# Modulation pieces, attention's small steps and buffer slots re-placed in a one-core hybrid block

## The chip, the cores and the metric

The kernel runs on one core of a Trainium2 chip. A core has a matrix engine (TensorE: PE for its matmuls, PEld for its weight loads), a vector engine (DVE), a scalar engine (ACT), GpSimd (POOL), and SyncE (SP), whose queue issues nearly all DMAs here. The metric is the device time of one execution, in microseconds (us); less is better.

## What is computed

One block of a hybrid model on 256 tokens of width 2048, in float32:

```python
mod = silu(c) @ ada_w + ada_b            # 6 x 2048: sh1, sc1, g1, sh2, sc2, g2
h = rmsnorm(x, norm1_g) * (1 + sc1) + sh1
z = h @ w_in                             # q, six k/v parts, gates, lx, ly, ga, gb
o_a = nsa_attention(q, ...)              # 16 heads, 4 kv groups, q * HEAD_DIM ** -0.5
o_b = gelu(ly) * rg_lru(causal_dwconv(lx), ...)
merged = sigmoid(ga) * (o_a @ proj_a) + sigmoid(gb) * (o_b @ proj_b)
x = x + g1 * (merged @ w_out)
h = rmsnorm(x, norm2_g) * (1 + sc2) + sh2
x = x + g2 * conv_glu_ffn(h, ffn_up, ..., ffn_down)
return rmsnorm(x, final_g)
```

Attention has three parts, weighted by sigmoid gates: over 15 compressed blocks, over selected blocks, and over a window. With 256 tokens the selection takes in all blocks and the window all tokens, so both are causal softmax attention with keys of their own.

## The kernel before, in words

**Dense products.** Every weight matrix comes in pieces of 128 x 2048 float32 (1 MB) into one of four `raw` buffers (`stage`, L97). `split` (L102) makes two halves of it, each as a rounded high part (ACT, L107) and the rest as a low part (DVE, L108), into `hi` and `lo` buffers of which there are three each. PE multiplies high by high, high by low and low by high. `dense_pair` (L114, matmuls L130), `dense_shift` (L135), `dense_pair1` (L172, matmuls L185, L187, L188) and `dense_tok` (L192, matmuls L203 to L205) are four forms of it. All loads go through `load` (L52) in program order on SP's queue, and a `raw` buffer is loaded again when DVE has read it.

**Modulation.** A column of `mod` for 128 outputs is the product of a 1 MB piece of the transposed `ada_w` with the row `crow`, summed over the row: one DVE instruction over 2048 elements. The first 32 pieces (sh1, sc1) are made at the start by `ada1_next` (L306, L323); the very first (`ada0`) is 32 small matmuls instead (L318). The other 64 stand in the list `fill` (L513: g1, then sc2, sh2, g2) and are taken off it by `filler` (L515), which runs `ada_piece` (L232: one load through a `raw` buffer, one product on DVE in L234, one addition in L235). Where the calls of `filler` stand in the program decides when that work comes.

```python
720  # lx loop, 8 passes:          filler(2)
773  # recurrence's gate, 8:       filler(2 if pr % 4 == 0 else 0)
797  # merge, n = 0..3, two sides: filler(2 if n == 0 else 4)
810  # behind merge:               filler(max(0, len(fill) - 16))
902  # feed-forward, first half:   filler(2 if gr > 5 else 1 if gr > 1 else 0)
```

**Stages, by time in the profile.** Norm and first columns (0 to 20 us); the projections for keys, values, queries and two gate blocks (L527 to L569, to about 240 us), whose outputs are collected in four spans of the contraction: the first span is copied out by ACT (L478), the others are added by DVE (L480); compression of keys and values (`gather`, `compress`); attention (L632), eight units of one group and one half of the tokens, between the last query projections and the lx loop (285 to 475 us); the recurrence with its gate (L725 to L773, to about 590 us); merge (L781 to L809): gates and two projections, four column tiles each; the output projection (L839 to L855, about 895 to 985 us), four tiles, each with its rows of x, a transposition and the scaled copies for the second norm; the feed-forward part.

**A unit of attention.** For the compressed part: scores, softmax in small DVE steps, transposition to `pcT` (L661). Then four heads, each: scores for both key sets in one PSUM tile `s` (two buffers, L667), the causal mask added by a matmul (L670), row maxima (DVE, L676), times -SCALE (L677), two exponentials on ACT with their sums (L679), the sums clamped (L681), inverted (L682) and times the gate (L683), the probabilities scaled (L686), turned by PE (L689) through one PSUM tile `tp` (tag "t", one buffer) and copied out by ACT (L691). At the end the products with the values (L693, L697) and the copy to `oA`.

**What orders the work.** The program is written stage by stage, but the order of the instructions on each engine is laid by a planner that simulates the program; `split` and `reduce` have raised priority. Tiles with the same tag share a slot, and a new tile waits for the last reader of the old one. `big` has slots B0, B1, C0 to C7, D0 to D5, M0 and M1; `tmp` has small ones (`xp`, `r`, `iu`, `u`, `tt`, `pv1`, `sm`).

Of the kernel before, what the change touches and what calls it, by code (L numbers as in the profile page):

```python
# [5 lines left out]
F32 = mybir.dt.float32  # L6
# [8 lines left out]
D = 2048  # L15
# [23 lines left out]
def block_kernel(tc, x_t, x_n, gf_row, cols_d, consts_d, ada_w, w_kv0, w_kv, w_v, w_gate, w_q, cmp_w, cmp_w2,  # L39
# [16 lines left out]
    with ExitStack() as es:  # L56
# [191 lines left out]
        ada0 = stage(ada_w[1, 0])  # L248
        ada1_raw = stage(ada_w[0, 0])
# [56 lines left out]
        def ada1_next():  # L306
            if not ada1:
                return
            with ExitStack() as behind:
# [4 lines left out]
                if kt == 0 and m == 1:  # L314

                    pa = psx.tile([128, 512], F32, tag="t", bufs=1, name="pa")
                    for j in range(KT):
                        PE.matmul(pa[:, 0:1], ada0[:, j * 128:j * 128 + 128], csil[:, j:j + 1], start=(j == 0),  # L318
                                  stop=(j == KT - 1))
# [38 lines left out]
        w2t = tmp.tile([128, 2, 128], F32, tag="xp", bufs=2, name="w2t")  # L358
# [22 lines left out]
        def gather(j, pos):  # L381

            parts = []
            for a in range(2):
                g = big.tile([128, 16, 4, NCMP], F32, tag="C6", name="gat")
# [3 lines left out]
                for n in range(2):  # L389
                    q = big.tile([128, 8, 2, 60], F32R, tag="C%d" % (2 + 2 * a + n), name="gath")  # L390
                    v = g[:, 8 * n:8 * n + 8].rearrange("p b g n -> p b (g n)")
                    A.activation(q[:, :, 0], v, AF.Copy)
                    V.tensor_tensor(q[:, :, 1], v, q[:, :, 0].bitcast(F32), op=ALU.subtract)
                    parts.append(q)
            return psx.tile([128, 512], F32, tag="s", bufs=2, name="cp"), parts

        def compress(j, cp, half):
# [16 lines left out]
            hs = tmp.tile([128, 4, 64], F32, tag="xp", bufs=2, name="hs")  # L414
# [21 lines left out]
        KV, TOK = range(4), range(8, 12)  # L436
# [31 lines left out]
        def out_of(i, ps, q):  # L468
            if i < 2 and q < 3:
                return  # L470
            for j in range(2):
# [5 lines left out]
                if q == 0 or i < 2:  # L477
                    A.activation(d, v, AF.Copy)  # L478
# [153 lines left out]
        def attention(g, t):  # L632
# [14 lines left out]
            A.activation(pc, pc, AF.Exp, scale=SCALE)  # L647
# [16 lines left out]
            nj = 2 * (t + 1)  # L664
            for hh in range(4):
# [5 lines left out]
                if hh == 0:  # L671
                    p = big.tile([128, 512], F32, tag="C3", name="p")
                else:
                    p = tmp.tile([128, 512], F32, tag=("r", "iu", "tt")[hh - 1], bufs=1, name="p")
                sm = tmp.tile([128, 6], F32, tag="sm", bufs=2, name="sm")
                V.tensor_reduce(sm[:, 0:2], s[:, 0:2 * nk].rearrange("p (b n) -> p b n", b=2), axis=AX, op=ALU.max)  # L676
                V.tensor_scalar(sm[:, 0:2], sm[:, 0:2], -SCALE, None, op0=ALU.mult)  # L677
                for b in range(2):
                    A.activation(p[:, b * nk:b * nk + nk], s[:, b * nk:b * nk + nk], AF.Exp, bias=sm[:, b:b + 1],  # L679
                                 scale=SCALE, accum_out=sm[:, 2 + b:3 + b])  # L680
                V.tensor_scalar(sm[:, 2:4], sm[:, 2:4], 1e-30, None, op0=ALU.max)  # L681
                V.reciprocal(sm[:, 2:4], sm[:, 2:4])  # L682
                V.tensor_tensor(sm[:, 4:6], sm[:, 2:4], gates[:, hh, 1:3], op=ALU.mult)  # L683
                for b in range(2):
                    pb = p[:, b * nk:b * nk + nk]
                    V.tensor_scalar(pb, pb, sm[:, 4 + b:5 + b], None, op0=ALU.mult)  # L686
                tp = psx.tile([128, 512], F32, tag="t", bufs=1, name="tp")
                for j in range(nj):
                    PE.transpose(tp[:, j * 128:j * 128 + 128], p[:, j * 128:j * 128 + 128], ident)  # L689
                for n in range(t + 1):  # L690
                    A.activation(pT[n][:, :, hh, :], tp[:, n * 256:n * 256 + 256].rearrange("p (j q) -> p j q", q=128),  # L691
                                 AF.Copy)
# [21 lines left out]
        for pr in range(8):  # L714
# [5 lines left out]
            filler(2)  # L720
# [4 lines left out]
        for bt in range(4):  # L725
# [37 lines left out]
            for h in range(2):  # L763
# [9 lines left out]
                filler(2 if pr % 4 == 0 else 0)  # L773
# [7 lines left out]
        for n in range(4):  # L781
            m = []
            for s, rhs in ((0, lambda kt: oA[:, kt]), (1, lambda kt: oB[kt // 2][:, kt % 2])):
# [3 lines left out]
                else:  # L787
                    ps = dense_tok([w_gates[n - 1, s, k] for k in range(4)], h1r)
# [4 lines left out]
                ps = dense_tok([w_proj[n, s, k] for k in range(4)], rhs)  # L793
# [3 lines left out]
                filler(2 if n == 0 else 4)  # L797
# [12 lines left out]
        filler(max(0, len(fill) - 16))  # L810
# [12 lines left out]
        for n in range(8):  # L823
            sh = modc[:, 48 + 2 * n:50 + 2 * n].unsqueeze(2).to_broadcast([128, 2, 2])
            A.activation(hp[n][:, :, 0, 256:258], sh, AF.Copy)
            V.tensor_tensor(hp[n][:, :, 1, 256:258], sh, hp[n][:, :, 0, 256:258].bitcast(F32), op=ALU.subtract)

# [11 lines left out]
        for n in range(4):  # L839
            ps = dense_tok([w_out[n, k] for k in range(4)], lambda kt: mg[kt // 2][:, kt % 2])  # L840
# [13 lines left out]
            if n == 1:  # L854
                tc.keep_in_program_order(A.activation(warm, col("eps"), AF.Sqrt))  # L855
        rstd(sdev, sums)
        dr = tmp.tile([128, 2, 128], F32, tag="xp", bufs=2, name="dr")
# [16 lines left out]
        for half in range(2):  # L874
# [3 lines left out]
            for gr in range(12):  # L878
                take = up(gr, 0, half)
                for f in range(2):  # L880
                    b = half * 24 + gr * 2 + f
                    gp = tmp.tile([128, 256], F32, tag="xp", bufs=2, name="gp")
# [137 lines left out]
```

## Time and profile before

| | us |
|---|---|
| median of 3 runs | 1792.68 |
| lowest, highest | 1792.08, 1794.26 |
| the profiled execution | 1793.77 |
| its span in the profile, first to last instruction | 1792.0 |
| PE busy | 1771.6 (99%) |
| PEld, DVE, ACT busy | 1545.9 (86%), 1350.5 (75%), 881.9 (49%) |
| read from HBM | 425.72 MB, 239 GB/s over the span |

Busy time is the time in which at least one instruction of an engine runs. Matmuls are pipelined: a row's duration is longer than the distance to the next start, and it is that distance (the pitch) that tells how fast PE goes. A wait is put down to the instruction that came last.

### The profile page before, as it was taken

What the parts mean: (1) busy time and instruction counts of PE and PEld (TensorE: products, weight loads), DVE (VectorE), ACT (ScalarE), POOL (GpSimd) and SP (SyncE); (2) the same over time, 40 slices, a digit from 0 to 9 for tenths busy, and PEclk for the clock granted to TensorE, in tenths of its full rate; (3) what the DMA queues carried; (4) which work ended last, traced back from release to release, by engine and by line L of the source; (5) the groups of instructions that cost most, each with busy time, mean ns of one, the idle gap of its engine ahead of it and who ended that gap; (6) DMA issues with size and microseconds to landing.
All of it is one profiled execution on the core that took longest, in us unless ns stands there. A gap on an engine that the chain in (4) does not pass through costs nothing.

```text
span 1792.0 us, 25746 instructions
## 1 busy us (share of the span) xinstructions
PE 1771.6 (99%) x10262; PEld 1545.9 (86%) x10262; DVE 1350.5 (75%) x1976; ACT 881.9 (49%) x1202; POOL 0.2 (0%) x4
## 2 busy tenths in 40 slices
PE   8999999999999999999999999999999999999997
PEld 7999898888999888888888998888888888888886
DVE  7998897998698766767765997888555677766555
ACT  5644464655578444444445644444433444444443
POOL 0000000000000000000000000000000000000000
PEclk9999999999999999999999999999999999999999
DMA  9999864665646867777775566777655555555552
GB/s 350 379 335 355 288 245 161 235 212 203 221 173 227 303 237 290 286 292 281 294 266 195 186 235 235 282 282 282 239 193 200 191 188 188 188 188 188 190 198 106
DMA packets 64200, 429.50 MB, mean 240 GB/s; under 512 B 7088, under 2 KB 7376, under 8 KB 15568
## 3 DMA queue, kind: packets, MB, share of 16 engines
q1 hardware_dynamic: 63792, 427.08, 66.2%
q8 instruction: 80, 1.31, 0.3%
q10 hardware_dynamic: 288, 0.79, 0.1%
q14 instruction: 40, 0.33, 0.1%
HBM read 425.72 MB, written 2.11 MB: 239 GB/s over the span
## 4 chain that ended last, share of the span: by engine, by line
PE 86%; DVE 6%; DMA 4%; issue 2%; ACT 2%; SPq 0%; DVEq 0%; ACTq 0%
PE P L130 26%; PE P L204 12%; PE P L205 12%; PE P L203 12%; PE P L187 3%; PE P L188 3%; PE P L185 3%; DMA raw<-ada_w 2%; DVE lo L108 2%; PE P L464 2%; PE P L466 2%; PE P L465 2%; PE P L149 1%; PE P L148 1%; PE P L150 1%
## 5 line engine op out<-in xcount | busy, mean ns | idle before, releaser
L107 ACT ACTIVATE hi<-raw 128x1024 fp32r<-128x1024 f32 x588 | 622.0, 1060 | 764.5 <-PE P L205 325.5
L108 DVE TENSOR_TENSOR lo<-raw,hi 128x1024 fp32r<-128x1024 f32 x588 | 717.1, 1222 | 370.5 <-ACT hi L107 369.7
L130 PE MATMUL P<-h,hi 128*128 128x512 f32 x1344 | 463.9, 394 | 0.0
L130 PE MATMUL P<-h,lo 128*128 128x256 f32 x1344 | 366.4, 278 | 0.0
L130 PEld LDWEIGHTS P<-h,hi 128*128 128x128 f32 x1344 | 249.1, 188 | 54.9
L130 PEld LDWEIGHTS P<-h,lo 128*128 128x128 f32 x1344 | 252.4, 188 | 4.2
L234 DVE SCALAR_TENSOR_TENSOR raw<-raw,crow 128x2048 f32<-128x2048 f32 x64 | 146.2, 2285 | 3.6 <-DMA raw<-ada_w 3.2
L188 PE MATMUL P<-h,lo 128*128 128x256 f32 x512 | 147.6, 289 | 0.8 <-DVE lo L108 0.8
L187 PE MATMUL P<-h,hi 128*128 128x256 f32 x512 | 146.7, 287 | 0.0
L185 PE MATMUL P<-h,hi 128*128 128x256 f32 x512 | 146.7, 287 | 0.0
L464 PE MATMUL P<-h,hi 128*128 128x256 f32 x384 | 107.9, 285 | 0.3 <-ACT hi L107 0.3
L465 PE MATMUL P<-h,hi 128*128 128x256 f32 x384 | 107.6, 284 | 0.0
L466 PE MATMUL P<-h,lo 128*128 128x256 f32 x384 | 102.2, 284 | 0.0
L188 PEld LDWEIGHTS P<-h,lo 128*128 128x128 f32 x512 | 97.8, 191 | 1.8 <-DVE lo L108 1.4
L187 PEld LDWEIGHTS P<-h,hi 128*128 128x128 f32 x512 | 97.9, 191 | 1.4 <-issue 1.2
L185 PEld LDWEIGHTS P<-h,hi 128*128 128x128 f32 x512 | 97.9, 191 | 1.0 <-issue 0.7
L204 PE MATMUL P<-lo,ua 128*128 128x512 f32 x240 | 93.5, 390 | 0.3 <-DVE lo L108 0.3
L205 PE MATMUL P<-hi,ua 128*128 128x512 f32 x240 | 93.4, 389 | 0.0
L203 PE MATMUL P<-hi,ua 128*128 128x512 f32 x240 | 83.6, 389 | 0.0
L204 PE MATMUL P<-lo,h 128*128 128x512 f32 x192 | 75.5, 393 | 0.0
L464 PEld LDWEIGHTS P<-h,hi 128*128 128x128 f32 x384 | 74.0, 193 | 1.1 <-ACT hi L107 0.5
L205 PE MATMUL P<-hi,h 128*128 128x512 f32 x192 | 74.9, 390 | 0.0
(281 smaller groups left out, 3131.6 us busy)
## 6 DMA issues: line engine op xcount, KB each, us to landing
raw<-ada_w SPq DMA_DIRECT2D x96, 1024.0 KB, 5.0
raw<-w_up SPq DMA_DIRECT2D x96, 1024.0 KB, 4.8
raw<-w_down SPq DMA_DIRECT2D x48, 1024.0 KB, 4.9
raw<-w_lru SPq DMA_DIRECT2D x32, 1024.0 KB, 4.9
raw<-w_proj SPq DMA_DIRECT2D x32, 1024.0 KB, 5.1
raw<-w_gates SPq DMA_DIRECT2D x24, 1024.0 KB, 6.5
raw<-w_out SPq DMA_DIRECT2D x16, 1024.0 KB, 4.9
raw<-w_kv SPq DMA_DIRECT2D x24, 512.0 KB, 6.7
```

Of the source, the lines that this page charges most:

```text
L107: A.activation(hi[:, :n], raw[:, lo_col:lo_col + n], AF.Copy)
L108: V.tensor_tensor(lo[:, :n], raw[:, lo_col:lo_col + n], hi[:, :n].bitcast(F32), op=ALU.subtract)
L130: PE.matmul(ps[f][:, 0:256] if w else ps[f], hl[w][:, k * 256 + f * 128:k * 256 + f * 128 + 128], r[:, 0:256] if w else r, start=(kt == 0 ...
L185: PE.matmul(o, hi[:, sl], r[:, 0:256], start=(kt == 0 and f == 0), stop=False, skip_group_check=True)
L187: PE.matmul(o, hi[:, sl], r[:, 256:512], start=False, stop=False, skip_group_check=True)
L188: PE.matmul(o, lo[:, sl], r[:, 0:256], start=False, stop=(kt == n - 1), skip_group_check=True)
L203: PE.matmul(ps[j], xh, hi[:, w], start=(kt == 0), stop=False, skip_group_check=True)
L204: PE.matmul(ps[j], xh, lo[:, w], start=False, stop=False, skip_group_check=True)
L205: PE.matmul(ps[j], xl, hi[:, w], start=False, stop=(kt == n - 1), skip_group_check=True)
L234: V.scalar_tensor_tensor(raw, raw, 1.0, row, op0=ALU.mult, op1=ALU.mult, accum_out=modc[:, c:c + 1])
L464: PE.matmul(o, hi[:, sl], h1[:, kt, 0:256], start=first and f % 2 == 0, stop=False, skip_group_check=True)
L465: PE.matmul(o, hi[:, sl], h1[:, kt, 256:512], start=False, stop=False, skip_group_check=True)
```

## The change

- `ada0` and `ada1_raw` no longer use `raw` buffers: they get D0, D1 and D5 (the slots of the first queries and of the values), and `ada0` is loaded in two halves.
- `cmpb`, `gat` and `gath` change slots; `w2t` and `hs` become the two halves of one tile, as do the two `gp` of the feed-forward part (tag "xp", now one buffer of the same total size).
- Queries are multiplied by SCALE as they are copied out; the factor leaves the three exponentials and the maxima, whose sign comes from the reduction.
- In attention the clamp, the inversion and the gate are done for two heads at a time, and the scaling, turning and copying of both heads follows.
- `filler` is called elsewhere: `dense_tok` takes a list `fills` of piece numbers behind which one piece is made. The 64 pieces lie so, before and after: lx loop 16 and 4, recurrence's gate 4 and 0, merge 28 and 36, output projection 0 and 8, feed-forward part 16 and 16.
- The shift copies (L823 to L826) move behind the output projection's loop.

```diff
-        def dense_tok(pieces, lhs, late=None):
+        def dense_tok(pieces, lhs, late=None, fills=()):
...
                     for j in range(2):
                         products(j, k0, *hl)
+                if ip in fills:
+                    filler()
...
-        ada0 = stage(ada_w[1, 0])
-        ada1_raw = stage(ada_w[0, 0])
+        ada0 = [big.tile([128, 1024], F32, tag="D%d" % n, name="ada0") for n in range(2)]
+        for n in range(2):
+            load(ada0[n], ada_w[1, 0][:, 1024 * n:1024 * n + 1024])
+        ada1_raw = big.tile([128, 2048], F32, tag="D5", name="ada1")
+        load(ada1_raw, ada_w[0, 0])
...
-        cmpb = big.tile([128, 1024], F32R, tag="C7", name="cmpb")
+        cmpb = big.tile([128, 1024], F32R, tag="C3", name="cmpb")
...
-                g = big.tile([128, 16, 4, NCMP], F32, tag="C6", name="gat")
+                g = big.tile([128, 16, 4, NCMP], F32, tag="C7", name="gat")
...
-                    q = big.tile([128, 8, 2, 60], F32R, tag="C%d" % (2 + 2 * a + n), name="gath")
+                    q = big.tile([128, 8, 2, 60], F32R, tag="C%d" % (2, 4, 5, 6)[2 * a + n], name="gath")
...
                 if q == 0 or i < 2:
-                    A.activation(d, v, AF.Copy)
+                    A.activation(d, v, AF.Copy, scale=SCALE if i in Q else 1.0)
+                elif i in Q:
+                    V.scalar_tensor_tensor(d, v, SCALE, d, op0=ALU.mult, op1=ALU.add)
                 else:
                     V.tensor_tensor(d, v, d, op=ALU.add)
...
+            sm = tmp.tile([128, 2, 4, 2], F32, tag="sm", bufs=2, name="sm")
+            heads = []
+
+            def turn_heads(hh):
+                p = heads[hh]
+                for b in range(2):
+                    pb = p[:, b * nk:b * nk + nk]
+                    V.tensor_scalar(pb, pb, sm[:, 1, hh, b:b + 1], None, op0=ALU.mult)
+                tp = psx.tile([128, 512], F32, tag="t", bufs=1, name="tp")
+                for j in range(nj):
+                    PE.transpose(tp[:, j * 128:j * 128 + 128], p[:, j * 128:j * 128 + 128], ident)
...
-                if hh == 0:
-                    p = big.tile([128, 512], F32, tag="C3", name="p")
-                else:
-                    p = tmp.tile([128, 512], F32, tag=("r", "iu", "tt")[hh - 1], bufs=1, name="p")
-                sm = tmp.tile([128, 6], F32, tag="sm", bufs=2, name="sm")
-                V.tensor_reduce(sm[:, 0:2], s[:, 0:2 * nk].rearrange("p (b n) -> p b n", b=2), axis=AX, op=ALU.max)
-                V.tensor_scalar(sm[:, 0:2], sm[:, 0:2], -SCALE, None, op0=ALU.mult)
+                p = tmp.tile([128, 512], F32, tag=("xp", "r", "iu", "tt")[hh], bufs=1, name="p")
+                V.tensor_reduce(sm[:, 0, hh], s[:, 0:2 * nk].rearrange("p (b n) -> p b n", b=2), axis=AX, op=ALU.max,
+                                negate=True)
...
+                heads.append(p)
+                if hh % 2 == 0:
+                    continue
+                w = sm[:, 1, hh - 1:hh + 1]
+                V.tensor_scalar(w, w, 1e-30, None, op0=ALU.max)
+                V.reciprocal(w, w)
+                V.tensor_tensor(w, w, gates[:, hh - 1:hh + 1, 1:3], op=ALU.mult)
+                turn_heads(hh - 1)
+                turn_heads(hh)
...
-            filler(2)
+            filler(pr % 2)
...
-                filler(2 if pr % 4 == 0 else 0)
...
-                    ps = dense_tok([w_gates[n - 1, s, k] for k in range(4)], h1r)
+                    ps = dense_tok([w_gates[n - 1, s, k] for k in range(4)], h1r, fills=(1, 3))
...
-                ps = dense_tok([w_proj[n, s, k] for k in range(4)], rhs)
+                ps = dense_tok([w_proj[n, s, k] for k in range(4)], rhs, fills=(0, 1, 3))
...
-                filler(2 if n == 0 else 4)
...
-            ps = dense_tok([w_out[n, k] for k in range(4)], lambda kt: mg[kt // 2][:, kt % 2])
+            ps = dense_tok([w_out[n, k] for k in range(4)], lambda kt: mg[kt // 2][:, kt % 2],
+                           fills=(0, 1, 3) if n < 2 else (0, 2) if n == 2 else ())
```

## Rows read from the trace of the kernel before

**Rows 1.** The page: busy time by engine (section 1) and the costliest groups (section 5).
```profile
PE 1771.6 (99%) x10262; PEld 1545.9 (86%) x10262; DVE 1350.5 (75%) x1976; ACT 881.9 (49%) x1202; POOL 0.2 (0%) x4
...
L108 DVE TENSOR_TENSOR lo<-raw,hi 128x1024 fp32r<-128x1024 f32 x588 | 717.1, 1222 | 370.5 <-ACT hi L107 369.7
```
**Rows 2.** Busy us by stretch: PE, PEld, DVE, ACT, POOL, clock, DMA share, GB/s.
```profile
50.00:150.00 100.00, 99.37 (x704) 93.58 (x703) 94.96 (x100) 53.27 (x76) 0.00 (x0) 1.00 0.96 359
285.00:475.00 190.00, 189.50 (x1306) 160.59 (x1305) 165.26 (x446) 109.94 (x267) 0.00 (x0) 1.00 0.56 200
...
890.00:915.00 25.00, 25.00 (x116) 20.61 (x115) 16.54 (x25) 11.40 (x16) 0.00 (x0) 1.00 0.93 362
915.00:965.00 50.00, 50.00 (x230) 41.38 (x229) 32.18 (x40) 27.36 (x40) 0.00 (x0) 1.00 0.60 210
```
**Rows 3.** What PE's matmuls waited for, whole span: us, times, longest.
```profile
PE hold L464 <- ACT h L292: 2.5, 2, 1.4
PE P L458 <- DVE lo L108: 1.4, 2, 1.0
PE P L188 <- DVE lo L108: 0.8, 2, 0.7
PE P L457 <- ACT hi L107: 0.7, 1, 0.7
PE tp L689 <- ACT pcT L661: 0.5, 1, 0.5
```
**Rows 4.** Timeline in the lx loop, PE: start, duration, instruction.
```profile
459.49 0.60 PE L689 MATMUL tp<-cols,p 128*128 128x128 f32 x4
...
459.84 0.36 PE L188 MATMUL P<-h,lo 128*128 128x256 f32 x1
...
460.04 0.28 PE L185 MATMUL P<-h,hi 128*128 128x256 f32 x1
...
460.16 0.28 PE L187 MATMUL P<-h,hi 128*128 128x256 f32 x1
```
**Rows 5.** Timeline in merge, PE.
```profile
800.25 0.39 PE L205 MATMUL P<-hi,oB 128*128 128x512 f32 x1
...
800.47 0.39 PE L203 MATMUL P<-hi,oB 128*128 128x512 f32 x1
```
**Rows 6.** DVE's groups by form, 280 to 480 us: busy us, mean ns.
```profile
L234 DVE SCALAR_TENSOR_TENSOR raw<-raw,crow 128x2048 f32<-128x2048 f32 x18 | 41.2, 2286 | 2.4 <-DMA raw<-ada_w 2.0
...
L681 DVE TENSOR_SCALAR sm<-sm 128x2 f32<-128x2 f32 x32 | 5.2, 162 | 3.3 <-ACT p L679 3.2
L682 DVE RECIPROCAL sm<-sm 128x2 f32<-128x2 f32 x32 | 5.1, 160 | 0.3
L677 DVE TENSOR_SCALAR sm<-sm 128x2 f32<-128x2 f32 x32 | 5.1, 161 | 0.1
L683 DVE TENSOR_TENSOR sm<-sm,gsig 128x2 f32<-128x2 f32 x32 | 5.0, 155 | 0.3
```
**Rows 7.** Groups by line, whole span.
```profile
L743 DVE SCALAR_TENSOR_TENSOR lt<-lx,cols,lt 128x253 f32<-128x253 f32 (+2 forms) x48 | 21.1, 473 | 0.0
...
L898 DVE TENSOR_TENSOR fv<-fv,fgl 128x256 f32<-128x256 f32 x48 | 18.2, 417 | 0.0
```
**Rows 8.** Timeline at the start: SP's queue, DVE, ACT.
```profile
5.60 13.68 SPq L53 DMA_DIRECT2D raw<-ada_w  x2
...
25.16 2.29 DVE L323 SCALAR_TENSOR_TENSOR raw<-raw,crow 128x2048 f32<-128x2048 f32 x1
...
28.14 0.51 ACT L292 ACTIVATE h<-nt,modc 128x256 fp32r<-128x256 f32 x1 [1.35 <-DVE nt L298]
```
**Rows 9.** What DVE waited for, the row of the fillers.
```profile
DVE raw L234 <- DMA raw<-ada_w: 3.2, 6, 1.0
```
**Rows 10.** The shift copies: durations ns min/median/max, first and last start.
```profile
L825 ACT ACTIVATE hp<-modc x8: 186/187/209, 875.2 to 894.2; 128x4 fp32r<-128x4 f32 x8
...
L826 DVE TENSOR_TENSOR hp<-modc,hp x8: 149/156/158, 876.4 to 896.6; 128x4 fp32r<-128x4 f32 x8
```

More of the change, by code (lines that the diff above doesn't have):

```diff
@@ L317, in ada1_next @@
                     for j in range(KT):
-                        PE.matmul(pa[:, 0:1], ada0[:, j * 128:j * 128 + 128], csil[:, j:j + 1], start=(j == 0),
+                        PE.matmul(pa[:, 0:1], ada0[j // 8][:, j % 8 * 128:j % 8 * 128 + 128], csil[:, j:j + 1], start=(j == 0),
                                   stop=(j == KT - 1))
@@ L353, in block_kernel @@
         vN = big.tile([128, 2, 2, 512], F32, tag="D5", name="vN")
-        cmpb = big.tile([128, 1024], F32R, tag="C7", name="cmpb")
+        cmpb = big.tile([128, 1024], F32R, tag="C3", name="cmpb")
         vcmp = cmpb[0:47, 0:512]
         pcs = [cmpb[:, 512 + 256 * n:768 + 256 * n].rearrange("p (h c) -> p h c", h=4) for n in range(2)]
-        w2t = tmp.tile([128, 2, 128], F32, tag="xp", bufs=2, name="w2t")
+        wh = tmp.tile([128, 2, 256], F32, tag="xp", bufs=1, name="wh")
+        w2t = wh[:, 0].rearrange("p (j e) -> p j e", j=2)
         kcmp = small["gap5"][:, 0:60]
@@ L413, in compress @@
                 return
-            hs = tmp.tile([128, 4, 64], F32, tag="xp", bufs=2, name="hs")
+            hs = wh[:, 1].rearrange("p (g n) -> p g n", g=4)
             V.memset(hs, 0.0)
@@ L435, in block_kernel @@
         blocks += [(w_mq[i], mq[i]) for i in range(2)]
-        KV, TOK = range(4), range(8, 12)
+        KV, Q, TOK = range(4), range(4, 8), range(8, 12)
         def banks_of(i, q):
@@ L646, in attention @@
             V.tensor_tensor(pc, pc, st[:, 0:4].unsqueeze(2).to_broadcast([128, 4, NCMP]), op=ALU.subtract)
-            A.activation(pc, pc, AF.Exp, scale=SCALE)
+            A.activation(pc, pc, AF.Exp)
             V.tensor_tensor(pc, pc, c01[:, t], op=ALU.mult)
@@ L664, in attention @@
             nj = 2 * (t + 1)
+            sm = tmp.tile([128, 2, 4, 2], F32, tag="sm", bufs=2, name="sm")
[8 more added lines that the diff above has]
+                    PE.transpose(tp[:, j * 128:j * 128 + 128], p[:, j * 128:j * 128 + 128], ident)
+                for n in range(t + 1):
+                    A.activation(pT[n][:, :, hh, :], tp[:, n * 256:n * 256 + 256].rearrange("p (j q) -> p j q", q=128),
+                                 AF.Copy)
             for hh in range(4):
@@ L677, in attention @@
-                V.tensor_scalar(sm[:, 0:2], sm[:, 0:2], -SCALE, None, op0=ALU.mult)
-                for b in range(2):
[L679 to L692, printed above, removed]
+                p = tmp.tile([128, 512], F32, tag=("xp", "r", "iu", "tt")[hh], bufs=1, name="p")
@@ new lines, in attention @@
+                V.tensor_reduce(sm[:, 0, hh], s[:, 0:2 * nk].rearrange("p (b n) -> p b n", b=2), axis=AX, op=ALU.max,
+                                negate=True)
+                for b in range(2):
+                    A.activation(p[:, b * nk:b * nk + nk], s[:, b * nk:b * nk + nk], AF.Exp, bias=sm[:, 0, hh, b:b + 1],
+                                 accum_out=sm[:, 1, hh, b:b + 1])
+                heads.append(p)
+                if hh % 2 == 0:
+                    continue
+                w = sm[:, 1, hh - 1:hh + 1]
@@ L809, in block_kernel @@
                 V.tensor_tensor(d[:, 256:512], p[:, 0:256], d[:, 0:256].bitcast(F32), op=ALU.subtract)
-        filler(max(0, len(fill) - 16))
+        assert len(fill) == 24
         V.scalar_tensor_tensor(modc[:, 64:80], modc[:, 64:80], 1.0, col("g2", 0, 16), op0=ALU.add, op1=ALU.mult)
@@ L822, in block_kernel @@
         sdev = small["sdev"]
[L823 to L826, printed above, removed]
         def add_rows(ps, j, n, row):
@@ L855, in block_kernel @@
                 tc.keep_in_program_order(A.activation(warm, col("eps"), AF.Sqrt))
+        for n in range(8):
+            sh = modc[:, 48 + 2 * n:50 + 2 * n].unsqueeze(2).to_broadcast([128, 2, 2])
+            A.activation(hp[n][:, :, 0, 256:258], sh, AF.Copy)
+            V.tensor_tensor(hp[n][:, :, 1, 256:258], sh, hp[n][:, :, 0, 256:258].bitcast(F32), op=ALU.subtract)
         rstd(sdev, sums)
-        dr = tmp.tile([128, 2, 128], F32, tag="xp", bufs=2, name="dr")
+        dr = tmp.tile([128, 2, 128], F32, tag="xp", bufs=1, name="dr")
         for j in range(2):
@@ L881, in block_kernel @@
                     b = half * 24 + gr * 2 + f
-                    gp = tmp.tile([128, 256], F32, tag="xp", bufs=2, name="gp")
+                    gps = tmp.tile([128, 2, 256], F32, tag="xp", bufs=1, name="gp") if f == 0 else gps
+                    gp = gps[:, f]
                     take(gp, f)
```

## The prediction

> **What bounds the kernel now.** I read the profile in this order: busy times, then the same by stage, then the waits of TensorE, then single matmuls in the timeline. The page gives PE as busy for 1771.6 of 1792.0 us [rows 1]; that alone proves little, since matmuls overlap. The stages say the same of each stretch: 189.50 of 190 us while attention runs (285 to 475 us), 50.00 of 50 in the output projection [rows 2]. The decisive view is what PE waited for: after its first matmuls, the largest entries of the whole run are 2.5 us for h (L292), 1.4 us for lo halves in the token-major blocks, 0.8 us for lo in the recurrence branch, 0.7 us for hi and 0.5 us for the pcT copy [rows 3]. Together that is 5.9 us. Of these entries only two lie wholly in the attention and recurrence stages, the 0.8 and the 0.5: 1.3 us. Last, the pitch at which matmuls start: 0.12 us for 256 columns in the recurrence branch [rows 4], 0.22 to 0.23 us for 512 columns in the merge [rows 5], with 96 of them (2 x 48) to a tile of four weight pieces: 21.8 us at 0.227. The change leaves every matmul in place, so nearly all of the span is work that it doesn't touch, and the prize is a few microseconds of waiting.
>
> One more cost is visible in the timeline. Behind a run of attention's own matmuls the next dense matmul takes 0.20 us instead of 0.12: the first one after four turns starts at 459.84, its successor at 460.04, the next at 460.16 [rows 4]. I counted some 80 such runs between 283 and 600 us; at 0.08 us each that is 6 to 7 us, paid per run and not per instruction of another engine.
>
> [...]
>
> **The change, part by part.** The sum is made against the profiled execution: 1793.77 us, of which 1792.0 are the span. The median of the three runs is 1792.68, 1.09 lower.
>
> *Modulation out of the lru stage.* Fillers before: 2 per pair in the lx loop (16) and 4 in the gate loop; after: one in every second lx pair (4), none later. So 16 of 20 leave, each 2.286 us on DVE [rows 6], some 2.5 us with the two short instructions behind it: 40 us of DVE, and 16 transfers of 1 MB on SP's queue. *Attention's small steps.* L677 goes (32 x 0.161 = 5.2 us, its sign now comes from the reduction and its factor from the queries); L681 to L683 run for two heads at a time, so half of 5.2 + 5.1 + 5.0 goes, 7.6 us [rows 6]. DVE in the stage falls from 165.26 of 190 us [rows 2] to about 165 - 13 - 35 = 117 (14 of the fillers removed lie in it). That is a large relief of an engine that PE waits for only 0.8 us [rows 3]; the 0.5 us wait is for ACT, which keeps its exponentials. The gain lies between 0 and 1.3 us. I take 0.8, the part that names DVE. The number of matmul runs stays: the turned heads still go through a single PSUM buffer (tag "t"), so ACT's copy separates the two heads' transposes as before. I take 0 for it; if half of the 32 transpose runs joined, 16 x 0.08 = 1.3 us would go.
>
> *Queries scaled once.* 24 evictions on DVE become a scalar_tensor_tensor. The same pair of forms elsewhere is 473 ns for 253 elements against 417 ns for 256 [rows 7], about 0.06 us more, 1.4 us in all. It falls where DVE is 95% busy (94.96 of 100 us, 50 to 150 us) while PE still runs 99.37 [rows 2]: the hi/lo buffers cover it. I take 0, bounds 0 and +1.4. The factor on ACT's evictions is part of an instruction that is there anyway: 0.
>
> *The first two modulation loads leave the raw buffers.* Now SP's queue sits from 5.60 to 19.28 us on the second of two loads, because its raw slot is ada0's, and w_kv's second piece is behind it [rows 8]. After, both are issued at once. But what PE waits for next is h at 28.14, which waits for DVE: the modulation product of that load starts at 25.16, back to back behind the one before [rows 8]. An earlier landing moves it only if the order on DVE changes too. The next loads still wait for the same slots to be freed. Bounds: 0, and all of the two waits for h and the one for hi, 2.5 + 0.7 = 3.2 us. The second wait for h is 2.5 - 1.4 = 1.1 us [rows 3]; I take half, 0.5 us. Halving ada0's load in two changes nothing behind it.
>
> *Modulation into merge and output projection.* Merge: 28 pieces before, 36 after, spread inside the tiles instead of in bursts of 2 or 4 behind them; output projection: none before, 8 after (3, 3, 2, 0); the feed-forward part keeps 16. Merge has room: a pair of tiles (43.6 us of PE) with 5 pieces needs 13 MB, 313 GB/s, and the chip moved 359 GB/s from 50 to 150 us [rows 2]. The output projection is the tight place. Its first two tiles then need 14 pieces of 1.049 MB, the 1.049 MB row of gate factors and two loads of x of 0.524 MB: 16.8 MB in 43.6 us, 385 GB/s. At 362 GB/s, what 890 to 915 us show [rows 2], that takes 46.4 us, 2.8 more; what the four raw buffers hold ahead covers some of it. DVE there is 32.18 of 50 us busy [rows 2]; over two tiles of some 22.5 us (with their transposes) that is 29.0, and six fillers add 15: 44 of 45. A filler now also stands in front of the next lo halves (1222 ns each [rows 1]) on DVE; should its load be late, they are late, and PE behind them. Before, fillers waited 3.2 us for loads in six waits, at most 1.0 [rows 9]. Nearest row for so full a pair of engines is 50 to 150 us: DMA 0.96, DVE 95%, PE 99.37 [rows 2]. I take 0, bounds 0 and +2.8.
>
> [...]
>
> *Moved and renamed pieces.* The 16 small shift copies (8 x 0.187 on ACT, 8 x 0.156 on DVE [rows 10]) are now written behind the projection's loop, and the first matmul of the feed-forward part reads them. Their input is ready when the third tile is under way, and before, they ran as soon as it was (875 to 897 us). I take 0; all in a row at the end would be 2.7 us. The other slots (cmpb to C3, the pair of gate buffers in one tile) change who waits for whom only where PE has other matmuls: 0.
>
> Sum: -0.8 - 0.5 = -1.3 us, 1792.5 for a run like the profiled one and **1791.4** against the median.
>
> **The rivals.**
> *A, the forecast*: PE is full, DVE's relief is idle time on DVE. 1791.4 us.
> *B, faster*: PE's order is laid by a planner; with DVE free it finds a better one, at the start and in attention. All bounds together: 3.2 + 1.3 + 1.3 = 5.8 us, 1786.9. [...] Against it: rows 3 has only 1.3 us there.
> *C, slower*: output projection with DVE at 98% and DMA at its rate. Eight fillers that each wait the longest wait seen, 1.0 us [rows 9], with lo behind them, add 8 us: 1791.4 + 8 = 1799.4. It decides from about 0.6 us per filler on (5 us against the 1.3 won). Against it: 50 to 150 us ran so full without loss.
> *D, slower*: a pair's turns stand where the planner puts them, now behind two more exponentials; if each of 16 pairs stops PE as the pcT copy did, 0.5 us [rows 3], 8 us come: 1799.4.
> That the change doesn't do what it says (the planner moves the new fillers to where the old ones were) gives A's time again.
>
> **How the numbers follow.** A measurement here can tell about 0.2%, 3.6 us: faster is below 1789.1, slower above 1796.3. A 0.57, B 0.27, C 0.11, D 0.05. The range reaches to B's time and a little below, and above over A with the unknown costs (+1.4 and +2.8) into C's smaller sizes: 1786.5 to 1797. A alone would be 1788.5 to 1794.5. Left out are the far ends of C and D and little of B.
>
> **What would show it.** Right: PE waits between 285 and 600 us under 1 us, DVE there near 60%, PE's pitch unchanged, SP's early wait gone, eight fillers between 890 and 960 us with PE still waiting for next to nothing. B would show as the wait for h gone and fewer intervals of 0.20 us. C: waits of PE for lo, and of fillers for loads, behind 890 us. D: PE waits on transposes. Wrong altogether would be a change in the pitch, or in the matmuls' count.

## The result, and the profile after

| | before | after |
|---|---|---|
| median, us | 1792.72 | 1805.52 |
| lowest to highest, four runs each | 1792.08 to 1794.26 | 1799.96 to 1809.19 |
| profiled execution, and its span | 1793.77, 1792.0 | 1805.49, 1803.7 |

The ratio is 1.0067, 95% interval 1.0041 to 1.0094: 12.8 us slower, where 1.3 us less was forecast and the range ended at 1797. The runs also spread over 9 us instead of 2.

The page of the changed kernel, busy times and the group of the modulation products (to be held against [rows 1] and the filler's row in [rows 6]):

```profile
PE 1776.8 (99%) x10262; PEld 1547.0 (86%) x10262; DVE 1345.3 (75%) x1896; ACT 885.1 (49%) x1204; POOL 0.2 (0%) x4
...
L237 DVE SCALAR_TENSOR_TENSOR raw<-raw,crow 128x2048 f32<-128x2048 f32 x64 | 146.5, 2289 | 74.6 <-DMA raw<-ada_w 74.5
```

The matmuls are as many as before, and PE's busy time grew by 5 us only. What is new stands in the last line: DVE stood idle for 74.5 us in front of the modulation product (now L237), waiting for the product's own load, against 3.2 us before [rows 9].

Where the time went is told by three marks in the timeline of PE's matmuls: attention's first score, the last matmul of the recurrence's dense products (L185), the feed-forward part's first (L148).

| us | before | after |
|---|---|---|
| attention's first score | 287.2 | 287.6 |
| from there to the recurrence's last product | 297.6 | 303.0 (+5.4) |
| from there, through merge and output projection, to the feed-forward part | 399.2 | 404.9 (+5.7) |
| from there to PE's last matmul | 798.9 | 799.2 |

So there are two losses, each of 5 to 6 us, and next to nothing elsewhere. The first sits in the recurrence, behind attention. PE's waits there, after, 285 to 595 us (us, times, longest):

```profile
PE P L185 <- ACT hi L107: 2.4, 1, 2.4
PE P L188 <- DVE lo L108: 1.5, 2, 1.1
PE s L692 <- ACT p L700: 0.7, 1, 0.7
```

The 2.4 us is one event. ACT's timeline of the kernel before:

```profile
511.77 1.11 ACT L107 ACTIVATE hi<-raw 128x1024 fp32r<-128x1024 f32 x1
513.44 0.63 ACT L755 ACTIVATE lt<-lt 128x512 f32<-128x512 f32 x1 [0.56 <-DVE lt L753]
513.98 1.04 ACT L107 ACTIVATE hi<-raw 128x1024 fp32r<-128x1024 f32 x1
515.04 1.28 ACT L756 ACT_TABLE_LOAD   x1
```

And of the changed kernel, with PE's view of the same stretch in the second fence:

```profile
512.14 1.10 ACT L107 ACTIVATE hi<-raw 128x1024 fp32r<-128x1024 f32 x1
513.81 0.63 ACT L773 ACTIVATE lt<-lt 128x512 f32<-128x512 f32 x1 [0.56 <-DVE lt L771]
514.46 1.28 ACT L774 ACT_TABLE_LOAD   x1
515.75 1.06 ACT L774 ACTIVATE lt<-lt 128x1024 f32<-128x1024 f32 x1
516.82 1.28 ACT L775 ACT_TABLE_LOAD   x1
518.11 1.06 ACT L775 ACTIVATE lt<-lt 128x1024 f32<-128x1024 f32 x1
519.08 1.99 ACT L107 ACTIVATE hi<-raw 128x1024 fp32r<-128x1024 f32 x2
```
```profile
517.50 0.28 PE L187 MATMUL P<-h,hi 128*128 128x256 f32 x1
520.17 0.38 PE L185 MATMUL P<-h,hi 128*128 128x256 f32 x1 [2.39 <-ACT hi L107]
...
521.69 0.41 PE L187 MATMUL P<-h,hi 128*128 128x256 f32 x1
521.90 0.41 PE L188 MATMUL P<-h,lo 128*128 128x256 f32 x1
```

Before, the planner put two high halves ahead of the exponential and the root with their table loads; after, only one. The second comes at 519.08; the last matmul that PE had work for began at 517.50. And it does not end with the wait: from 521.5 to 524.5 us the pitch is 0.21 us and not the 0.12 of [rows 4]. The view by stretches says why; its clock column reads 0.73 and 0.59 in two stretches of 2.5 us and is back at 1.00 from 525 us on (columns as in [rows 2]):

```profile
517.50:520.00 2.50, 0.28 (x3) 0.08 (x1) 2.49 (x6) 2.49 (x3) 0.00 (x0) 1.00 0.48 108
520.00:522.50 2.50, 2.33 (x14) 2.33 (x15) 2.50 (x5) 1.07 (x2) 0.00 (x0) 0.73 0.76 318
522.50:525.00 2.50, 2.50 (x14) 2.47 (x13) 2.12 (x2) 0.30 (x1) 0.00 (x0) 0.59 0.29 39
525.00:530.00 5.00, 5.00 (x37) 4.74 (x35) 3.57 (x5) 3.57 (x4) 0.00 (x0) 1.00 0.46 190
```

The second loss lies in merge and output projection. What PE, DVE and SP's queue waited for there, after (PE and DVE from 595 to 1005 us, SP from 590 to 1000; the last fence is SP before):

```profile
PE P L205 <- DVE lo L108: 2.4, 7, 0.5
```
```profile
DVE raw L237 <- DMA raw<-ada_w: 69.7, 37, 3.2
DVE lo L108 <- ACT hi L107: 32.1, 32, 2.0
```
```profile
SPq L53 <- DVE raw L237: 217.1, 43, 7.1
SPq L53 <- DVE lo L108: 119.5, 47, 5.5
```
```profile
SPq L53 <- DVE raw L234: 29.8, 16, 2.2
```

Before, PE and the products had no wait here that the views list. PE's 2.4 us are less than the 5.7 lost, because a wait is counted from the recorded end of the matmul before it, and that lies 0.39 us behind its start where the next one would have started after 0.227 us [rows 5]: each of the seven waits stands for some 0.16 us more, 3.5 us together. The rest is in delays that the view does not list.

One such wait in the timeline, with what it does to PE:

```profile
845.08 1.06 ACT L107 ACTIVATE hi<-raw 128x1024 fp32r<-128x1024 f32 x1 [1.66 <-PE P L206]
...
847.80 1.07 ACT L107 ACTIVATE hi<-raw 128x1024 fp32r<-128x1024 f32 x1 [1.66 <-PE P L206]
847.89 2.29 DVE L237 SCALAR_TENSOR_TENSOR raw<-raw,crow 128x2048 f32<-128x2048 f32 x1 [3.20 <-DMA raw<-ada_w]
...
850.10 1.22 DVE L108 TENSOR_TENSOR lo<-raw,hi 128x1024 fp32r<-128x1024 f32 x1
...
851.38 0.50 PE L205 MATMUL P<-lo,oA 128*128 128x512 f32 x1 [0.44 <-DVE lo L108]
```

DVE stands for 3.20 us, works 2.29 us on the modulation piece, and only then makes the low half whose high half ACT began at 845.08; PE stops for it. The queue's view closes the circle: SP waits 217.1 us for a product of L237 to give a raw buffer back, and that product waits for a load that SP could only issue late. The stretches after, beside [rows 2], and then the merge's before:

```profile
285.00:475.00 190.00, 189.28 (x1308) 160.53 (x1308) 132.16 (x329) 110.70 (x267) 0.00 (x0) 1.00 0.38 135
...
580.00:890.00 310.00, 306.75 (x1391) 252.02 (x1390) 232.69 (x262) 133.82 (x145) 0.00 (x0) 1.00 0.81 304
890.00:915.00 25.00, 24.98 (x112) 20.45 (x111) 18.90 (x24) 10.38 (x14) 0.00 (x0) 1.00 0.92 340
915.00:965.00 50.00, 49.70 (x227) 40.70 (x227) 44.12 (x59) 24.43 (x37) 0.00 (x0) 1.00 0.93 360
```
```profile
580.00:890.00 310.00, 310.00 (x1399) 256.94 (x1398) 217.69 (x238) 131.89 (x147) 0.00 (x0) 1.00 0.77 280
```

Merge lost PE time at 304 GB/s and a DMA share of 0.81; the output projection, at 360 GB/s and with DVE 88% busy, lost little.

### The profile page after: what moved, and what is told of

It reads as the page before. It is cut to its first block, busy times and chain, and to the rows that moved or that the text cites. A ratio compares the mean times of both kernels' runs of the same rounds, so it can differ in the third digit from the quotient of the medians.

```text
span 1803.7 us, 25620 instructions
## 1 busy us (share of the span) xinstructions
PE 1776.8 (99%) x10262; PEld 1547.0 (86%) x10262; DVE 1345.3 (75%) x1896; ACT 885.1 (49%) x1204; POOL 0.2 (0%) x4
## 4 chain that ended last, share of the span: by engine, by line
PE 71%; DMA 15%; DVE 8%; issue 3%; ACT 3%; SPq 0%; DVEq 0%; ACTq 0%
PE P L130 26%; DMA raw<-ada_w 12%; PE P L205 6%; PE P L206 6%; PE P L204 6%; DVE raw L237 4%; PE P L187 2%; PE P L185 2%; PE P L188 2%; PE P L472 2%; PE P L473 2%; PE P L474 2%; DVE lo L108 2%; DMA raw<-w_kv 1%; PE P L149 1%
## 5 line engine op out<-in xcount | busy, mean ns | idle before, releaser
L237 DVE SCALAR_TENSOR_TENSOR raw<-raw,crow 128x2048 f32<-128x2048 f32 x64 | 146.5, 2289 | 74.6 <-DMA raw<-ada_w 74.5
L185 PE MATMUL P<-h,hi 128*128 128x256 f32 x512 | 147.1, 287 | 2.4 <-ACT hi L107 2.4
L185 PEld LDWEIGHTS P<-h,hi 128*128 128x128 f32 x512 | 98.7, 193 | 3.5 <-ACT hi L107 2.6
```

What stands on the lines that cost most here:

```text
L185: PE.matmul(o, hi[:, sl], r[:, 0:256], start=(kt == 0 and f == 0), stop=False, skip_group_check=True)
L237: V.scalar_tensor_tensor(raw, raw, 1.0, row, op0=ALU.mult, op1=ALU.mult, accum_out=modc[:, c:c + 1])
```

## The experiments

For each run the table gives the median beside that of the kernel before in the same session, the ratio with its 95% interval, and the two inner stretches of the table above in its profile.

| run | us | before | ratio | to recurrence's end | merge and projection |
|---|---|---|---|---|---|
| before | | | | 297.6 | 399.2 |
| after | 1805.52 | 1792.72 | 1.0067 (1.0041 to 1.0094) | 303.0 | 404.9 |
| e1_places | 1804.26 | 1793.29 | 1.0056 (1.0041 to 1.0071) | 301.8 | 407.5 |
| e2_old_places | 1796.35 | 1793.29 | 1.0017 (1.0007 to 1.0026) | 298.2 | 399.8 |
| e3_load_ahead | 1800.24 | 1793.29 | 1.0035 (1.0022 to 1.0049) | 301.8 | 401.6 |
| e4_spread_old_count | 1796.80 | 1793.29 | 1.0022 (1.0013 to 1.0032) | 298.2 | 402.4 |
| e5_bursts_new_count | 1821.25 | 1794.20 | 1.0144 (1.0128 to 1.0160) | 302.6 | 420.9 |
| e6_no_wait | 1801.32 | 1794.20 | 1.0039 (1.0024 to 1.0054) | 301.4 | 398.9 |
| e7_no_load | 1800.71 | 1794.20 | 1.0035 (1.0022 to 1.0047) | 301.5 | 399.4 |
| e8_old_start | 1795.52 | 1794.20 | 1.0006 (0.9997 to 1.0015) | 298.1 | 400.3 |
| e9_start_only | 1794.44 | 1793.70 | 1.0004 (0.9995 to 1.0013) | 297.6 | 399.5 |
| e10_gate_out | 1794.01 | 1793.70 | 0.9998 (0.9989 to 1.0007) | 298.2 | 399.3 |
| e11_lx_out | 1795.23 | 1793.70 | 1.0007 (0.9998 to 1.0016) | 297.9 | 399.6 |
| e12_both_out | 1797.38 | 1793.70 | 1.0020 (1.0010 to 1.0029) | 300.3 | 399.0 |

**The change cut in two.** First the kernel before with only the modulation's places changed, as in the diff above (`fills` in `dense_tok` and its calls, the calls of `filler`, the shift copies):

```diff
-            filler(2)
+            filler(pr % 2)
...
-                filler(2 if pr % 4 == 0 else 0)
...
-                ps = dense_tok([w_proj[n, s, k] for k in range(4)], rhs)
+                ps = dense_tok([w_proj[n, s, k] for k in range(4)], rhs, fills=(0, 1, 3))
```

> The kernel before with only the modulation pieces placed as after the change (and the shift copies behind the projection). Theory 'fillers wait' (a piece's product stands on DVE in front of the next lo halves and waits for its own load): the merge and projection loss of 5.7 us is all here; the time is 1798 to 1800 us, DVE waits about 70 us for ada_w loads behind 590 us (0.3 us before). Rival 'steps and slots' (attention's new steps and slots make the planner's order worse): 1792 to 1794 us, nothing of the loss. The recurrence's loss of 5.4 us (a wait of 2.4 us for hi behind two table loads) is open: if it comes from the places, this run has it too and reads 1803 to 1806 us.

1804.26 us: the places alone carry 11.0 of the 12.8 us, and both losses, the wait of 2.4 us for hi included. DVE waits 71.8 us for modulation loads behind 595 us.

Then the reverse, the changed kernel with the old places:

```diff
-            filler(pr % 2)
+            filler(2)
...
+                filler(2 if pr % 4 == 0 else 0)
...
-                ps = dense_tok([w_proj[n, s, k] for k in range(4)], rhs, fills=(0, 1, 3))
+                ps = dense_tok([w_proj[n, s, k] for k in range(4)], rhs)
...
                 m.append(sg)
+                filler(2 if n == 0 else 4)
```

> The changed kernel with the modulation pieces back where they were before; attention's steps, scaled queries and slots stay. 'Fillers wait': 1791 to 1794 us if the recurrence's loss also comes from the places, 1796 to 1799 us if that one comes from steps and slots. Rival 'steps and slots': 1800 us or more.

1796.35 us, both losses gone from the profile (298.2 and 399.8). Attention's steps, the scaled queries and the slots bring nothing; with the start they cost 3 us. The time lies in the range that was given for a recurrence's loss from steps and slots, but that loss isn't there: the range was met by these 3 us, which were not expected.

**Merge and projection.** Is it the wait, the volume, or DVE's time? The first test keeps volume and places and issues a piece's load one weight piece earlier:

```diff
+                ahead = filler_load() if ip in fills else None
                 raw = stage(ap)
...
-                if ip in fills:
-                    filler()
+                if ahead:
+                    ahead()
```

> The changed kernel; in merge and output projection a modulation piece is loaded before the weight piece of its place and not behind it, its product on DVE stays behind that weight piece's lo halves. Volume, number of products and places are the same. 'Fillers wait': DVE's wait for ada_w behind 590 us falls from 70 us to under 15, PE's waits for lo there from 2.9 us to under 1, and 4 to 6 us come back: 1799 to 1802 us. Rival 'volume' (36 and 8 pieces are too many transfers for these stages): no change, 1803 to 1808 us, waits move to the weights' loads.

1800.24 us; the stretch falls from 404.9 to 401.6, 3.3 us of the 5.7. DVE's wait only falls from 69.7 to 40.6 us, not below 15 as expected, and PE's waits for lo to 1.0. With four buffers in rotation an earlier place in the queue is not a load as much earlier: SP still waits 188.7 us for these products to give a buffer back (217.1 in the changed kernel). Places, volume and DVE's work are the changed kernel's here; only the waiting is less, and the loss is less with it.

The next two replace the product's operand. From the second merge column on it reads the row twice, in halves, into a free slot; in the one the piece is still loaded, in the other it isn't:

```diff
+        def filler_apart():
+            m, kt = fill.pop(0)
+            c = m * 16 + kt
+            stage(ada_w[m, kt])
+            for n in range(2):
+                V.scalar_tensor_tensor(apart[n], crow[:, 1024 * n:1024 * n + 1024], 1.0, crow[:, 1024 * n:1024 * n + 1024],
+                                       op0=ALU.mult, op1=ALU.mult, accum_out=modc[:, c:c + 1])
...
                 if ip in fills:
-                    filler()
+                    (filler_apart if apart else filler)()
```

> The changed kernel, but from the second merge column on (30 pieces of merge, 8 of the projection) a piece is loaded as before and its product on DVE reads the row twice instead of the loaded piece (two halves of 1024, about 2.4 us together, into a slot of its own); those columns of the modulation are therefore not the reference's. Same transfers, same DVE time, no wait for the load. 'Fillers wait': PE's waits for lo behind 640 us under 0.5 us, the loss between 640 us and the projection's end under 1 us (5.5 us in the changed kernel); 1799 to 1802 us. 'Volume': the loss stays and moves to hi behind loads of weights; 1803 us or more.

> As the run before this one, without the loads (38 pieces are not read at all; those columns are not the reference's). Same DVE time, 40 MB less. 'Fillers wait' and 'volume' both expect the loss behind 640 us gone, 1799 to 1802 us. Theory 'DVE time' (the products themselves, in front of lo, are too long): the loss stays, 1803 us or more, with PE's waits for lo as they were.

398.9 and 399.4 us: the loss of this stretch is gone in both, and PE's view lists no wait there. The first of the two kept all transfers in their places. The products did not keep theirs: with no load to wait for, the planner laid all 38 between 647 and 815 us (in the changed kernel they go on to 957). There DVE was busy all the time, and PE as well; the changed kernel's row, then that of the run with the loads:

```profile
650.00:815.00 165.00, 164.07 (x723) 133.64 (x722) 118.54 (x129) 70.30 (x75) 0.00 (x0) 1.00 0.81 308
```
```profile
650.00:815.00 165.00, 165.00 (x734) 136.50 (x733) 164.69 (x266) 71.27 (x75) 0.00 (x0) 1.00 0.80 308
```

So at the same 308 GB/s and with 46 us more of DVE's work PE lost nothing in this stretch: neither the rate nor DVE's time is what costs. What both runs took away is the product's wait for its load. Two limits: the products' places changed with it, and a loaded piece that nothing reads has no product for SP to wait for before it loads the buffer again, so the run takes away both ends of the circle, DVE's wait (5.2 us for ada_w behind 595 us, 69.7 in the changed kernel) and SP's wait for DVE. That less waiting with the places kept also gives time back, the run before these showed.

Is it the spreading? The pieces in bursts behind the tiles, as before, with the new counts:

```diff
-                ps = dense_tok([w_proj[n, s, k] for k in range(4)], rhs, fills=(0, 1, 3))
+                ps = dense_tok([w_proj[n, s, k] for k in range(4)], rhs)
...
                 m.append(sg)
+                filler(3 if n == 0 else 5)
```

> The changed kernel with its counts per stage (4, 0, 36, 8) but the pieces of merge and projection in bursts behind the tiles (3 or 5 behind each side of a merge tile; 3, 3, 2 behind the projection's tiles). The volume of each stage is the changed kernel's. Theory 'fillers wait' because spread: most of the merge and projection loss (5.7 us) goes, 1799 to 1801 us; what is left is the recurrence's. Rival 'volume': the loss stays, 1803 to 1807 us.

1821.25 us, outside of both expectations. Here not the products wait but the weights behind a burst. ACT's waits from 595 to 1025 us:

```profile
ACT hi L107 <- PE P L206: 175.9, 113, 7.1
ACT hi L107 <- DMA raw<-w_gates: 33.9, 9, 7.5
```

In the kernel before, that second row was 12.7 us and PE listed no wait. Not all of the loss is waiting: behind four of PE's waits the granted clock was 0.66 over 5 us (from 727, 775, 823 and 918 us), by an estimate from these figures 4 x 5 x 0.34 = 6.8 us. That five pieces in a row are too many for four raw buffers is the likely reason; it was not tested apart. For so many pieces spreading is thus the better way (ratio 1.0067 against 1.0144). The counterpart keeps the spreading and goes back to the old counts (lx loop 16, gate loop 4, merge 28, behind the second and fourth piece):

```diff
-            filler(pr % 2)
+            filler(2)
...
+                filler(2 if pr % 4 == 0 else 0)
...
-                ps = dense_tok([w_proj[n, s, k] for k in range(4)], rhs, fills=(0, 1, 3))
+                ps = dense_tok([w_proj[n, s, k] for k in range(4)], rhs, fills=(1, 3))
...
-                           fills=(0, 1, 3) if n < 2 else (0, 2) if n == 2 else ())
```

> The changed kernel with the counts of before (lx loop 16, recurrence's gate 4, merge 28, projection 0), but the merge's pieces spread inside its tiles, behind the second and fourth weight piece. 'Fillers wait': a piece behind the second weight piece still stands in front of lo halves and waits; merge loses 2 to 4 us against before. 'Volume': the loss in merge is gone (under 1 us). The recurrence's loss goes if it comes from the missing pieces there: 1794 to 1797 us in all; 1799 to 1803 us if it stays.

1796.80 us, 0.45 above the run with the old places; DVE's wait for modulation loads is 18.7 us instead of 69.7. By the medians spreading alone costs under 1 us, as rival 'volume' had it, and not the 2 to 4 us of 'fillers wait'. So the loss comes with the number of pieces, though not by the rate: it is with more of them that the products wait for loads. The profiled execution was the slowest of its ten, with 402.4 us in the stretch. One event is enough for that: PE waits 1.7 us at 590.75 us for a lo half, in front of which DVE had a modulation product and four steps of the recurrence, and behind it the granted clock is 0.67 from 590 to 595 us, by an estimate from these figures some 1.7 us more (5 x 0.33).

**The recurrence.** In the runs with the new places its stretch is 301.4 to 303.0 us with the wait of 2.4 us for hi; in those with the old ones it is near 298. Three kernels are the one before with pieces left out: the gate loop's 4, the lx loop's 12, and both.

```diff
-                filler(2 if pr % 4 == 0 else 0)
+                del fill[:2 if pr % 4 == 0 else 0]
...
-            filler(2)
+            filler(pr % 2)
+            del fill[:2 - pr % 2]
```

> The kernel before without the 4 modulation pieces of the recurrence's gate loop (not loaded, not computed, their columns set to zero). 'Missing pieces there let the planner put the hi of the next weight half behind the two table loads': PE waits 2.4 us for hi around 515 us and the merge begins 3 to 5 us later than in the kernel before; time 1795 to 1798 us. If the pieces of the lx loop are the cause: nothing of that, 1791 to 1794 us.

> The kernel before without 12 of the 16 modulation pieces of the lx loop (columns set to zero). 'Attention is relieved' (the gain that was forecast): PE's waits between 285 and 475 us fall from 1.3 us to 0.5 or less, 1790 to 1792 us. 'Relief is idle time': 1792 to 1794 us. If these pieces cause the recurrence's wait: 1795 to 1798 us with 2.4 us for hi.

> The kernel before without the 4 pieces of the gate loop and the 12 of the lx loop, all else in its place (columns set to zero). If missing pieces cause the recurrence's loss at all, it is here: 2.4 us for hi, merge 3 to 5 us late, 1795 to 1798 us. If not, 1790 to 1793 us, and the loss belongs to how the later places change the planner's order.

1794.01, 1795.23 and 1797.38 us. PE's waits from 285 to 595 us, without the lx pieces, and without both:

```profile
PE P L185 <- ACT hi L107: 0.7, 2, 0.4
PE P L204 <- DVE lo L108: 0.4, 1, 0.4
PE P L188 <- DVE lo L108: 0.2, 1, 0.2
```
```profile
PE P L185 <- ACT hi L107: 2.4, 1, 2.4
PE P L188 <- DVE lo L108: 1.2, 2, 0.8
```

Only with both sets missing is the wait there, without any other part of the change; either set alone keeps it away. So the loss comes from taking modulation away from attention and recurrence. The order on ACT is only half of it. Without the lx pieces alone, ACT too has just one high half ahead of the two table loads:

```profile
512.52 1.11 ACT L107 ACTIVATE hi<-raw 128x1024 fp32r<-128x1024 f32 x1
514.85 1.28 ACT L757 ACT_TABLE_LOAD   x1
517.21 1.28 ACT L758 ACT_TABLE_LOAD   x1
519.47 2.94 ACT L107 ACTIVATE hi<-raw 128x1024 fp32r<-128x1024 f32 x3
```

But there PE had one half more in stock: its run of dense matmuls goes on to 520.78 us, and to 517.72 with both sets missing, where the next high half begins at 519.29. (The run with the old places is like the former.) The wait needs both, the high half behind the tables and the shorter stock. Why the planner arrives at this was not traced. The run without the lx pieces also tests the forecast's gain: some 30 us less of DVE's work (12 x 2.5; from 285 to 475 us DVE is busy 142.06 us, 165.26 before), and no wait of PE is listed in that stretch any more, as was expected; yet the time is 1795.23 us against 1793.70, an interval that holds no change.

**The start.** Two runs: the old places and the old start, and the kernel before with the new start alone.

```diff
-        ada0 = stage(ada_w[1, 0])
-        ada1_raw = stage(ada_w[0, 0])
+        ada0 = [big.tile([128, 1024], F32, tag="D%d" % n, name="ada0") for n in range(2)]
```

> The run with the modulation pieces in their old places, and also the first two modulation loads back in raw buffers: attention's steps, scaled queries and the other slots stay. That run was 1796.35 us against 1793.29 before. Theory 'start' (loads that are now all issued at once share the DMA engines, so the first ones land later): 1793 to 1794 us, the wait for h back from 3.6 to 2.5 us. Rival 'steps': no change, 1796 us.

> The kernel before with only the first two modulation loads moved out of the raw buffers (into D0, D1, D5). Theory 'start' (all first loads issued at once share the DMA engines, h comes later, and the time varies more): 1794 to 1796 us, 1 to 2 us above the kernel before. Rival: 1792 to 1794 us, the same as before; then the 3 us that the changed steps and slots cost lie in attention's steps.

1795.52 (ratio 1.0006) and 1794.44 us (1.0004): both intervals hold 1. The runs do not tell the theories apart. That first loads land later, the traces of before and after show: in the first 30 us the four loads of w_kv took a median of 9.7 us from issue to landing before and 13.0 after, with the DMA engines 0.90 and 0.89 busy over that time; what it costs they do not show. Attention's first score comes between 285.9 and 290.0 us over all profiles and at 285.9 and 288.6 in two kernels with the same start, so a single profile says nothing here. How the 3 us of the second run (old places) divide between the start and attention's steps stays open.

## Why the prediction was wrong

*What bounds the kernel* held. PE's matmuls are as before, the feed-forward part takes the same 799 us, and the prize was small. The conclusion drawn from it did not: that there was little to win said nothing of what there was to lose.

*Modulation out of the lru stage and attention's small steps* were sized too large: DVE fell from 165.26 to 132.16 us of the 190, by 33 and not by 48 us. With the places alone (e1) it is 140.57, with the old places (e2) 156.81: 24.7 us of the 35, and 8.4 of the 13. "A large relief of an engine that PE waits for only 0.8 us" was the right reading; the gain of 0.8 us was not there.

*One more cost*, the 0.20 us behind attention's turns, was a misreading. In the trace the four turns of [rows 4] start at 459.49, 459.60, 459.70 and 459.81; the dense matmul is recorded only 0.03 us behind the last, and its successor 0.20 behind that. Together that is 0.23 us, just what a turn and a dense matmul take elsewhere (0.11 and 0.12). Behind turns nothing is lost, so the 1.3 us for joined turns in B's sum did not exist; the forecast itself took 0.

*The recurrence* is the first step that failed: "The gain lies between 0 and 1.3 us". The forecast gave a planner's new order a place only as a gain (B) or as turns of heads that come too late (D). What came was a third: with the pieces gone, the planner put a high half behind two table loads and left PE a shorter stock, +5.4 us. Of these 2.4 us are the wait; 1.4 us are the fallen clock behind it (15 matmuls at a pitch of 0.213 instead of 0.12 us); of the other 1.6, 0.9 are in smaller waits (for lo 1.5 us against 0.8, for `p` 0.7 where the pcT copy had 0.5), and the rest is not told apart.

*Modulation into merge* is the second. The step was that merge has room because its pieces need 313 GB/s and the chip had moved 359; it was put at 0, with at most 2.8 us for the projection. The rate was the wrong test. Merge ran at 304 GB/s and, with the projection, lost 5.7 us; e6 ran the same transfers without the wait and lost nothing. Half of the right terms stood a few sentences on, with the output projection: a filler stands in front of the lo halves. That four raw buffers decide how early its load can start was missing; they appear there only as a help. Rival C had this mechanism, with 8 waits of at most 1.0 us in the projection; it was 37 waits of up to 3.2 us, 34 of them in merge. C's time, 1799.4, comes near the changed kernel without the recurrence's loss (1805.5 - 5.4 = 1800.1), but by another sum.

*The output projection* cost 0.9 us of the 5.7 (its first matmul starts 10.54 us late, the feed-forward part 11.45), inside the bounds of 0 to 2.8. The upper one was worked out from the 362 GB/s of before, from 890 to 915 us [rows 2]. That rate decided nothing: merge lost at 304, and e6 moved 390 GB/s from 890 to 915 us without a wait of PE. Nor was 362 the most for a short stretch: the changed kernel moved 424 GB/s from 12 to 20 us.

*The start*: SP's wait of 13.68 us is gone, the first loads all go out by 11.5 us, and PE still waits 2.5 us for h. The 0.5 us was not won, for the reason given with the bound: DVE was the later one (the second product starts at 25.02 us, before at 25.16). *Queries scaled once, the slots*: no wait names them. The 24 evictions on DVE took a median of 683 ns before and after, not 0.06 us more, and ACT's eight 597 and 594 ns. Together with attention's steps they cost 1.3 us by the medians (e8, whose interval holds no change) and 3.1 with the start (e2), not taken apart. *The shift copies* moved with the places, and no wait names them.

In attention the weight loads were busy for 160.59 of the 190 us before [rows 2] and for 160.53 with DVE relieved, and PE won nothing: here pitch and waits decided, as the forecast took it.

## What to carry to other kernels

When work that waits for a transfer is moved onto an engine that also feeds the bottleneck, ask what stands behind it there (here a low half behind 3.20 us of waiting and 2.29 us of work on DVE) and how many buffers ago its load could start; the bandwidth of the stage does not answer that (from 650 to 815 us e6 had the changed kernel's 308 GB/s and lost nothing). Count buffers per piece of time, not bytes alone. Where a planner lays the order, taking work away can cost time too (3.7 us in e12), so before trusting a relief look at each engine's order around long steps, such as the table loads of 1.28 us here, and at how much work the engine behind has in stock when they begin.

## What was not expected of the hardware

A wait of PE of 2.4 us is not always paid once. In the changed kernel the granted clock was 0.73 and 0.59 in the two stretches of 2.5 us behind it, and 15 dense matmuls came at a pitch of 0.213 instead of 0.12 us, 1.4 us in all. The same wait of 2.4 us stands in seven profiles. In the changed kernel, e1 and e5 the clock fell with it (0.88, 0.86 and 0.86 from 512 to 524 us); in e3, e6, e7 and e12 it stayed at 1.00. The row of the changed kernel, then of e3 and of e12:

```profile
512.00:524.00 12.00, 9.61 (x70) 9.41 (x69) 11.99 (x22) 8.46 (x9) 0.00 (x0) 0.88 0.26 89
```
```profile
512.00:524.00 12.00, 9.61 (x76) 9.25 (x75) 11.99 (x20) 9.22 (x10) 0.00 (x0) 1.00 0.25 89
```
```profile
512.00:524.00 12.00, 9.62 (x78) 9.34 (x77) 11.99 (x23) 9.23 (x11) 0.00 (x0) 1.00 0.26 89
```

e3, e6 and e7 have the changed kernel's recurrence, and their stretch is 1.2 to 1.6 us shorter, which fits the 1.4. What decides between the three profiles and the four, these runs do not show. Waits of 1.1 to 1.7 us were followed by such a fall too (to 0.67 in e4 behind 590.75 us, to 0.66 four times in e5). Whether the clock is part of why the changed kernel's runs spread over 9 us was not tested; its mean over each of the four was 0.995 or 0.996.
